# New places in the on-chip memory for the forms of x, the values and the heads' output of a hybrid decoder layer, and one form computed and split later

## The chip, the cores and the metric

The kernel runs on one core of a Trainium2 chip. Its time is the device time in microseconds of one execution. TensorE (PE) multiplies matrices; its loads of the stationary operand have a row of their own in the profile (PEld). VectorE (DVE), ScalarE (ACT) and GpSimd (POOL) do the elementwise work, and SyncE (SP) and GpSimd start transfers. Operands of a matmul lie in the on-chip memory (SBUF), in 128 partitions; a tile's place is a byte address that is the same in every partition. This text counts such addresses in units of 64 bytes, which are 16 floats.

## The reference

One decoder layer on 512 tokens with 16 learned tokens ahead, model width 1024. All weights of the first projection are one matrix `w_in`.

```python
u = rms_norm(h, norm_gain)
proj = u @ w_in
(rq, rk, rv, rg, gq, gk, gv, gg, glr, m_ret, m_gla) = jnp.split(proj, points, axis=-1)
rq, rk = rope(rq), rope(rk) * 256 ** -0.5               # 4 heads of 256
o_ret = head_group_norm(retention_chunked(rq, rk, rv)) * silu(rg)     # 4 heads of 512
log_a = log_sigmoid(glr @ w_gate_up + b_gate) / 16
o_gla = head_rms_norm(gla_chunked(gq, gk, gv, log_a)) * silu(gg)      # 4 heads: keys 128, values 256
merged = sigmoid(m_ret) * (o_ret @ w_branch_ret) + sigmoid(m_gla) * (o_gla @ w_branch_gla)
return rms_norm(h + merged @ w_out, final_norm_gain)[:, N_META:]
```

(Reshapes are left out, and the gains of the norms.) The result is 512 x 1024 in float32.

## The kernel before

**Products in three matmuls.** A float32 operand is split into a high part, which ScalarE makes by a cast (`split`, L154), and a low part, which VectorE makes by subtracting the high part from the value. A product of two operands is the sum of high by high, high by low and low by high: three matmuls with the same result tile (`mm3`, L189 to L193, and the inner loop of `quad`, L318).

**Seven products for eight.** `quad` computes a product of a 2x2 block matrix of x (two halves of tokens `th` by two halves of the width `kh`) with a 2x2 block of weights by seven block products. They are issued in the order 1, 2, 6, 7, 5, 4, 3 and use the forms A11, A12, S2, S3, S1, A22, S4 of x: three are blocks of x itself, and S1 to S4 are sums and differences of blocks. Each product is 24 matmuls: two halves of 128 columns, four blocks of depth, three matmuls each. With `rows=True` a form of x is the stationary operand and 256 columns of a weight are the moving one; this holds for `gv1`, `gg0`, `gg1`, `rg0` to `rg3`, `rv0` to `rv3` (gates and values of the heads) and `wo1` (a part of the output projection). With `rows=False` the weight is stationary and the form moves, 256 or, where the learned tokens go along, 264 columns; this holds for `rqk0` to `rqk3` and `gqk1` (queries and keys), `mr0`, `mr1`, `mg0`, `mg1` (merging gates) and `bg0`, `bg1` (the GLA branch, whose forms come from the GLA heads and not from x). The projections `gq0`, `gk0` and `gv0` are done with all eight products, and so are two other parts of the output projection, `wo0` and `wo2`, with the merged heads as stationary operand.

**Where the operands lie.** `xh` and `xl` hold the high and low parts of x, one tile per `kh`, shaped [128, 4, 2, 272]: four blocks of depth, two halves of tokens, 264 columns used of 272. A row (one block of depth) is 34 units of 64 bytes, and the second half starts 17 units behind the first. S1 to S4 lie in tiles `fh3` to `fh6` and `fl3` to `fl6` of [128, 4, 272], with rows of 17 units. A split weight is [128, 4, 256], rows of 16 units, in one of three buffers each for high and low (`whi`, `wlo`); raw weights come by transfers into six buffers. Values of a retention head are `vh` and `vl`, its gates `sg`, the scores `sh` and `sl`, its normed and gated output, transposed, `oh` and `ol`; the branch projection (`br`, 512 wide) has weights stationary and `oh`, `ol` moving. The merged heads `mh`, `ml` take over tiles that are free by then, and their forms those of `fh3` to `fl6`.

**Order.** A scheduler places each instruction on its engine, and the code fixes the order where it matters: `pin` ties each product on TensorE to the last one before it; `act` and `vec` do the same on ScalarE and VectorE; `after` names one predecessor. Stages are generators that `weave` interleaves, a step of the dense one (a product) with a step of another chain. `low` holds the last cast and subtraction of a weight. In `gla_g(0)` (the quad `gg0`) the GLA heads' chain of small matmuls runs between the products. The forms of x are made once, at the start: in `forget_gates` (from L754) S2 and S4 are cast, then all four low parts are subtracted.

Of the kernel before, what the change touches and what calls it, by code (L numbers as in the profile page):

```python
# [28 lines left out]
P = 128  # L29
D = 1024  # L30
T = 512
# [16 lines left out]
E_U, E_D, E_A, E_B, E_END, E_ND = range(6)  # L48
A11, A12, A22, S1, S2, S3, S4 = range(7)


# [57 lines left out]
def hybrid_kernel(ctx: ExitStack, tc: tile.TileContext, I, out: bass.AP):  # L109
# [18 lines left out]

    xh = [cp.tile([P, 4, 2, HW], F32R, tag=f"xh{i}", name=f"xh{i}") for i in range(2)]
    xl = [cp.tile([P, 4, 2, HW], F32R, tag=f"xl{i}", name=f"xl{i}") for i in range(2)]  # L130
    ah = {(th, kh): xh[kh][:, :, th] for th in range(2) for kh in range(2)}
    al = {(th, kh): xl[kh][:, :, th] for th in range(2) for kh in range(2)}
    fh = [ah[0, 0], ah[0, 1], ah[1, 1]]
    fl = [al[0, 0], al[0, 1], al[1, 1]]
    fh += [cp.tile([P, 4, HW], F32R, tag=f"fh{i}", name=f"fh{i}") for i in range(3, 7)]
    fl += [cp.tile([P, 4, HW], F32R, tag=f"fl{i}", name=f"fl{i}") for i in range(3, 7)]

# [27 lines left out]
    def act(ins):  # L165
        return queue("act", ins)

    def vec(ins):
        return queue("vec", ins)
# [493 lines left out]
    for n in range(NTB):  # L663
        act(nc.scalar.activation(xr[n], xr[n], AF.Square, accum_out=ss[:, n:n + 1]))
        if n == 2:
            for s in range(2):
# [14 lines left out]
                             rt.unsqueeze(2).to_broadcast([P, NTB + 1, P])))  # L681
    vec(nc.vector.scalar_tensor_tensor(u01, u00, -1.0, u01, op0=ALU.mult, op1=ALU.subtract))

    def form(i, x):
        act(nc.scalar.copy(fh[i][:, :, :HT], x))

        def rest():
            vec(nc.vector.tensor_sub(fl[i][:, :, :HT], x, fh[i][:, :, :HT].bitcast(F32)))

        return rest  # L690
# [40 lines left out]
    def forget_gates():  # L731
# [24 lines left out]
        next_weights(0)  # L756
        forms.append(form(S4, u01))
        for i in (2, 0, 1, 3):
            forms[i]()
        yield  # L760
        def values(p):
# [84 lines left out]
    def gla_g(p):  # L846
        sg = g1.tile([P, NTB, 512], F32, tag="gsg", name=f"gsg{p}")
        G["sg", p] = sg

        def evac(n, th, x, y):  # L850
            total(sg[:, 2 * th:2 * th + 2, n * 256:(n + 1) * 256], x, y)

        yield from quad((C_GG + p * 512, C_GG + p * 512 + 256), True, f"gg{p}", evac,
                        sooner=p == 0)

# [408 lines left out]
    def ret_g(h):  # L1264
        sg = rp.tile([P, NTB, 512], F32, tag="sg", name=f"sg{h}")
        R["sg", h] = sg
# [3 lines left out]
    def ret_v(h):  # L1270
        vh = rp.tile([P, NTB, 512], F32R, tag="vh", name=f"vh{h}")
        vl = rp.tile([P, NTB, 512], F32R, tag="vl", name=f"vl{h}")
        R["v", h] = vh, vl
# [23 lines left out]
    def ret_scores(h):  # L1297
        qh, ql, kh, kl = R["qk", h]
        dec = rp.tile([P, 2, T], F32, tag="dec", name=f"dec{h}")
        nc.sync.dma_start(dec, I["decay"][h])  # L1300
        sh = rp.tile([P, 1280], F32R, tag="sh", name=f"sh{h}")
        sl = rp.tile([P, 1280], F32R, tag="sl", name=f"sl{h}")
# [26 lines left out]
    def ret_attention(h):  # L1329
# [4 lines left out]
        if h == 0:  # L1334
            nc.gpsimd.memset(rp.tile([P, 16], F32, name="gap"), 0.0)
        oh, ol = [(rp if h < 3 else cp).tile([P, 4, T], F32R, tag=f"o{n}" if h < 3 else f"x{n}0", name=f"o{n}{h}")
                  for n in "hl"]
        R["o", h] = oh, ol
# [109 lines left out]
    for h in range(4):  # L1448
# [10 lines left out]
        else:  # L1459
            weave(run(ret_g(h), ret_v(h)), run(every(ret_rope(h), 3, 2, at if h else None), ret_scores(h)))  # L1460
    weave(gates_ret(), ret_attention(3))

    mh, ml = [[cp.tile([P, 4, T], F32R, tag=f"x{n}1", name=f"m{n}0"),
               rp.tile([P, 4, T], F32R, tag=("sg", "vl")[n == "l"], name=f"m{n}1")] for n in "hl"]
    sums = [[cp.tile([P, 4, 256], F32R, tag=f"f{n}{i}", name=f"ms{n}{i}") for i in range(3, 7)] for n in "hl"]
    mforms = [[m[0][:, :, :256], m[1][:, :, :256], m[1][:, :, 256:], *x] for m, x in zip((mh, ml), sums)]

# [37 lines left out]

    weave(ret_branches(), residual(), skip=14)


# [105 lines left out]
```

## Time and profile before

| | |
|---|---|
| median of 3 runs | 757.08 us (756.8 to 758.7) |
| profiled execution, its own time | 759.11 us |
| span of the profiled execution | 757.3 us |
| granted TensorE clock in it | 0.998 |
| TensorE busy | 748.2 us, 99%, 5595 matmuls |
| VectorE busy | 609.2 us, 80% |
| ScalarE busy | 450.4 us, 59% |
| GpSimd busy | 138.8 us, 18% |
| read from and written to device memory | 104.44 and 11.53 MB |

Engines work side by side, so the shares don't add up. A busy time of TensorE counts a matmul from its issue to its modelled end, and matmuls overlap: the mean duration of a 128x256 matmul is given as 281 ns while 24 of them pass in 2.75 to 2.85 us. How fast matmuls follow each other is therefore read from the chain of waits, whose rows give start, length and number (`x24`) of a run of instructions with one name. That chain goes back from the last instruction, at each step to what released it. The columns of a window are its bounds and length, then the busy time and number of instructions of PE, PEld, DVE, ACT and POOL, the granted clock, the DMA engines' share and GB/s.

### The profile page before, as it was taken

To read this page: it belongs to the slowest core of one execution; us is meant where nothing else is said; L and a number is where in the kernel's file an instruction comes from. 1 tells how busy PE (TensorE), PEld (TensorE's weight loads), DVE (VectorE), ACT (ScalarE), POOL (GpSimd) and SP (SyncE) were. 2 spreads that over 40 slices of the span, in tenths; PEclk is the share of its full clock that TensorE was granted. 3 is DMA by queue.
4 is the path that set the end of the run, shared out by engine and by line. 5 is a ranking of instruction groups with operands and counts; after the bars stand their busy time and mean duration, and the time that the engine had idled before them with its cause. 6 is when DMAs were issued, how large, how long until landed. Compare 5 with 4: busy or idle time off the path is not lost.

```text
span 757.3 us, 14065 instructions
## 1 busy us (share of the span) xinstructions
PE 748.2 (99%) x5595; PEld 701.3 (93%) x5595; DVE 609.2 (80%) x873; ACT 450.4 (59%) x764; POOL 138.8 (18%) x173
## 2 busy tenths in 40 slices
PE   9999999999999999999999999999999999999996
PEld 6799899999999999999989999989999999988996
DVE  6699877679897789789957688966787989775994
ACT  7897584666974466556546555646464756532562
POOL 2211110101221122110530100440011210111142
PEclk9999999999999999999999999999999999999999
DMA  9863421821589972733783562795476356687503
GB/s 301 286 141 78 118 63 50 195 85 57 130 182 272 305 165 88 168 112 133 199 249 117 120 159 86 204 223 136 130 166 145 107 144 189 227 194 210 128 29 112
DMA packets 100138, 117.42 MB, mean 155 GB/s; under 512 B 5732, under 2 KB 90852, under 8 KB 99816
## 3 DMA queue, kind: packets, MB, share of 16 engines
q1 hardware_dynamic: 79896, 88.19, 36.7%
q0 software_dynamic: 19888, 27.79, 20.3%
q8 instruction: 44, 0.72, 0.4%
q10 hardware_dynamic: 288, 0.53, 0.2%
q14 instruction: 22, 0.18, 0.1%
HBM read 104.44 MB, written 11.53 MB: 153 GB/s over the span
## 4 chain that ended last, share of the span: by engine, by line
PE 86%; DVE 6%; ACT 2%; DMA 2%; issue 2%; POOL 1%; POOLq 0%; DVEq 0%; ACTq 0%
PE rqk_b L318 6%; PE rv_b L318 6%; PE rg_b L318 6%; PE rqk_c L318 5%; PE br_p L193 3%; PE br_p L189 3%; PE br_p L192 3%; PE gg_b L318 3%; PE gv_p L643 3%; PE mg_b L318 3%; PE rv_c L318 3%; PE rg_c L318 3%; PE mr_b L318 2%; PE bg_b L318 2%; PE gg_c L318 2%
## 5 line engine op out<-in xcount | busy, mean ns | idle before, releaser
L189 PE MATMUL br_p<-oh,br_h 128*128 128x512 f32 x128 | 50.0, 390 | 0.0
L193 PE MATMUL br_p<-oh,br_l 128*128 128x512 f32 x128 | 50.0, 390 | 0.0
L192 PE MATMUL br_p<-ol,br_h 128*128 128x512 f32 x128 | 49.8, 389 | 0.0
L154 ACT CAST rv_h<-rv_w 128x1024 fp32r<-128x1024 f32 x24 | 25.3, 1052 | 27.2 <-DVE rv_w L372 9.6
L154 DVE TENSOR_TENSOR rv_l<-rv_w,rv_h 128x1024 fp32r<-128x1024 f32 x24 | 29.3, 1221 | 9.2 <-ACT rv_h L154 9.2
L154 DVE TENSOR_TENSOR rg_l<-rg_w,rg_h 128x1024 fp32r<-128x1024 f32 x20 | 24.4, 1220 | 8.3 <-ACT rg_h L154 8.3
L154 ACT CAST rg_h<-rg_w 128x1024 fp32r<-128x1024 f32 x20 | 21.0, 1052 | 15.6 <-PE br_p L192 6.0
L282 POOL DMA_DIRECT2D rqk_x<-in_w_in_dram x8 | 10.4, 1302 | 105.4 <-DVE rv_l L154 80.6
L193 PEld LDWEIGHTS br_p<-oh,br_l 128*128 128x128 f32 x128 | 24.0, 188 | 5.2
L192 PEld LDWEIGHTS br_p<-ol,br_h 128*128 128x128 f32 x128 | 24.0, 188 | 4.7
L189 PEld LDWEIGHTS br_p<-oh,br_h 128*128 128x128 f32 x128 | 24.1, 188 | 4.5
L154 ACT CAST rqk_h<-rqk_w 128x1024 fp32r<-128x1024 f32 x20 | 21.1, 1053 | 11.5 <-PE rqk_c L318 2.9
L154 ACT CAST br_h<-br_w 128x1024 fp32r<-128x1024 f32 x16 | 16.8, 1050 | 18.7 <-PE br_p L192 9.5
L154 DVE TENSOR_TENSOR rqk_l<-rqk_w,rqk_h 128x1024 fp32r<-128x1024 f32 x20 | 24.4, 1221 | 3.9 <-ACT rqk_h L154 3.8
L1354 ACT ACTIVATE on<-av,nm,g_r 128x512 f32<-128x512 f32 x16 | 12.5, 779 | 25.3 <-DVE nm L1352 25.3
L318 PE MATMUL rv_b<-rv_l,fh 128*128 128x256 f32 x96 | 27.1, 282 | 0.2 <-DVE rv_l L154 0.2
L318 PE MATMUL rqk_b<-fh,rqk_h 128*128 128x256 f32 (+1 forms) x96 | 27.2, 283 | 0.0
L318 PE MATMUL rqk_b<-fh,rqk_l 128*128 128x256 f32 (+1 forms) x96 | 27.1, 282 | 0.0
L318 PE MATMUL rqk_b<-fl,rqk_h 128*128 128x256 f32 (+1 forms) x96 | 27.1, 282 | 0.0
L318 PE MATMUL rg_b<-rg_h,fl 128*128 128x256 f32 x96 | 27.0, 281 | 0.0
L318 PE MATMUL rv_b<-rv_h,fl 128*128 128x256 f32 x96 | 27.0, 281 | 0.0
L318 PE MATMUL rg_b<-rg_l,fh 128*128 128x256 f32 x96 | 26.9, 280 | 0.0
(721 smaller groups left out, 3260.8 us busy)
## 6 DMA issues: line engine op xcount, KB each, us to landing
rv_w<-in_w_in_dram SPq DMA_DIRECT2D x16, 512.0 KB, 4.2
br_w<-in_w_branch_ret_dram SPq DMA_DIRECT2D x16, 512.0 KB, 3.4
rqk_w<-in_w_in_dram SPq DMA_DIRECT2D x12, 512.0 KB, 4.8
rg_w<-in_w_in_dram SPq DMA_DIRECT2D x12, 512.0 KB, 4.5
rqk_x<-in_w_in_dram SPq DMA_DIRECT2D x8, 512.0 KB, 4.0
rqk_x<-in_w_in_dram POOLq DMA_DIRECT2D x8, 512.0 KB, 8.0
rg_x<-in_w_in_dram SPq DMA_DIRECT2D x8, 512.0 KB, 3.7
rg_x<-in_w_in_dram POOLq DMA_DIRECT2D x8, 512.0 KB, 7.8
```

What stands on the lines that cost most here:

```text
L154: return nc.scalar.copy(hi, src), nc.vector.tensor_sub(lo, src, hi.bitcast(F32))
L189: m = nc.tensor.matmul(o, lh, rh, start=first, stop=False)
L192: nc.tensor.matmul(o, lh, rl, start=False, stop=False)
L193: m = nc.tensor.matmul(o, ll, rh, start=False, stop=last)
L282: x = nc.gpsimd.dma_start(t, block(0, 1), accum_op=ALU.add)
L318: m = nc.tensor.matmul(ps[t][:, :n] if wide else ps[t], l, r, start=first and j == 0, stop=kk == 3 and j == 2, skip_group_check=not fresh ...
L643: m = nc.tensor.matmul(pss[t], (al if j == 1 else ah)[t // 2, kh][:, k, c], (lo if j == 2 else hi)[:, kk, :], start=q == kk == j == 0, sto ...
L1354: nc.scalar.activation(on, ps, AF.Identity, scale=r, bias=nm)
```

## The change

The forms of x move into three pairs of tiles. `x0` (rows of 544 floats, 34 units) holds the first half of the width, both halves of tokens 272 floats apart, and form S4 in columns 288 to 543: it lies on the second half of tokens of that block of x, which is not read any more when S4 is made. `x1` (rows of 864 floats, 54 units) holds the second half of the width, halves 288 floats apart, and S1 behind them. `x2` (rows of 608 floats, 38 units) holds S2 and S3, each 288 wide. Two tiles that hold nothing (`gap0`, 16 floats, `gap1`, 112 floats) shift what follows. In the built program the parts and forms that the quads read start at even units and split weights still start at odd ones. S1 and S4 are now 256 wide, where they were 264.

`sg` and `vl` become 2304 and 2176 floats instead of 2048, `sh` is read from 64 floats (256 bytes) on, the memset of a 16-float gap goes and the tile stays without it, and the last head's `oh`, `ol` go into the tiles of `x2`, 112 floats in. The merged heads and their forms get the same rows as x.

Form S4 is not made in `forget_gates` any more. There only its float32 value is computed, after the other forms were split; its cast and its subtraction come in `gla_g(0)`, behind the fifth product of `gg0`, tied to the cast and the subtraction of the weights last split. TensorE's and SyncE's instructions and their order stay as they were.

```diff
--- before.py
+++ after.py
@@ -47,6 +47,7 @@
 SOFF = (0, 512, 896, 1152)
 E_U, E_D, E_A, E_B, E_END, E_ND = range(6)
 A11, A12, A22, S1, S2, S3, S4 = range(7)
+OH3 = 112
 
 
 def constants():
@@ -126,14 +127,22 @@
     nc.gpsimd.memset(one, 1.0)
 
 
-    xh = [cp.tile([P, 4, 2, HW], F32R, tag=f"xh{i}", name=f"xh{i}") for i in range(2)]
-    xl = [cp.tile([P, 4, 2, HW], F32R, tag=f"xl{i}", name=f"xl{i}") for i in range(2)]
+    def gap(pool, n, name):
+        pool.tile([P, n], F32, name=name)
+
+    gap(cp, 16, "gap0")
+    x0, x1, x2 = [[cp.tile([P, 4, w], F32R, tag=f"x{n}{i}", name=f"x{n}{i}") for n in "hl"]
+                  for i, w in enumerate((544, 864, 608))]
+    gap(cp, 112, "gap1")
+
+    def halves(t, w):
+        return t[:, :, :2 * w].rearrange("p k (t c) -> p k t c", t=2)
+
+    xh, xl = [[halves(a, HW), halves(b, 288)] for a, b in zip(x0, x1)]
     ah = {(th, kh): xh[kh][:, :, th] for th in range(2) for kh in range(2)}
     al = {(th, kh): xl[kh][:, :, th] for th in range(2) for kh in range(2)}
-    fh = [ah[0, 0], ah[0, 1], ah[1, 1]]
-    fl = [al[0, 0], al[0, 1], al[1, 1]]
-    fh += [cp.tile([P, 4, HW], F32R, tag=f"fh{i}", name=f"fh{i}") for i in range(3, 7)]
-    fl += [cp.tile([P, 4, HW], F32R, tag=f"fl{i}", name=f"fl{i}") for i in range(3, 7)]
+    fh, fl = [[a[0, 0], a[0, 1], a[1, 1], b[:, :, 576:832], c[:, :, :288], c[:, :, 288:576], z[:, :, 288:]]
+              for a, z, b, c in zip((ah, al), x0, x1, x2)]
 
     rt = cp.tile([P, NTB + 1], F32, name="rt")
     rneg = cp.tile([P, NTB + 1], F32, name="rneg")
@@ -679,13 +688,22 @@
 
     vec(nc.vector.tensor_mul(dg, ident.unsqueeze(1).to_broadcast([P, NTB + 1, P]),
                              rt.unsqueeze(2).to_broadcast([P, NTB + 1, P])))
-    vec(nc.vector.scalar_tensor_tensor(u01, u00, -1.0, u01, op0=ALU.mult, op1=ALU.subtract))
-
-    def form(i, x):
-        act(nc.scalar.copy(fh[i][:, :, :HT], x))
+
+    def form(i, x, prev=None):
+        w = 256 if i in (S1, S4) else HT
+        h, l, x = fh[i][:, :, :w], fl[i][:, :, :w], x[:, :, :w]
+        y = nc.scalar.copy(h, x)
+        if prev:
+            after(y, prev[0])
+        else:
+            act(y)
 
         def rest():
-            vec(nc.vector.tensor_sub(fl[i][:, :, :HT], x, fh[i][:, :, :HT].bitcast(F32)))
+            y = nc.vector.tensor_sub(l, x, h.bitcast(F32))
+            if prev:
+                after(y, prev[1])
+            else:
+                vec(y)
 
         return rest
 
@@ -754,9 +772,9 @@
         parts["gk0", 0] = wsplit([P, 4, 256], "gk0_0")
         forms.append(form(S2, u00))
         next_weights(0)
-        forms.append(form(S4, u01))
-        for i in (2, 0, 1, 3):
+        for i in (2, 0, 1):
             forms[i]()
+        vec(nc.vector.scalar_tensor_tensor(u10, u00, -1.0, u01, op0=ALU.mult, op1=ALU.subtract))
         yield
         def values(p):
             for t in (2 * p, 2 * p + 1):
@@ -850,8 +868,13 @@
         def evac(n, th, x, y):
             total(sg[:, 2 * th:2 * th + 2, n * 256:(n + 1) * 256], x, y)
 
-        yield from quad((C_GG + p * 512, C_GG + p * 512 + 256), True, f"gg{p}", evac,
-                        sooner=p == 0)
+        products = quad((C_GG + p * 512, C_GG + p * 512 + 256), True, f"gg{p}", evac, sooner=p == 0)
+        if p == 0:
+            yield from islice(products, 4)
+            next(products)
+            form(S4, u10, low)()
+            yield
+        yield from products
 
     def gla_qk(p):
         q = gp.tile([P, 2, T], F32, tag="gq", name=f"gq{p}")
@@ -1262,14 +1285,14 @@
         yield
 
     def ret_g(h):
-        sg = rp.tile([P, NTB, 512], F32, tag="sg", name=f"sg{h}")
+        sg = rp.tile([P, 2304], F32, tag="sg", name=f"sg{h}")[:, :2048].rearrange("p (b c) -> p b c", b=NTB)
         R["sg", h] = sg
         yield from quad((C_RG + h * 512, C_RG + h * 512 + 256), True, f"rg{h}", rows_into(sg, AF.Silu),
                         ahead=h % 3 == 0, behind=R.get(("pow", h - 1)))
 
     def ret_v(h):
         vh = rp.tile([P, NTB, 512], F32R, tag="vh", name=f"vh{h}")
-        vl = rp.tile([P, NTB, 512], F32R, tag="vl", name=f"vl{h}")
+        vl = rp.tile([P, 2176], F32R, tag="vl", name=f"vl{h}")[:, :2048].rearrange("p (b c) -> p b c", b=NTB)
         R["v", h] = vh, vl
 
         def meta(psm):
@@ -1298,7 +1321,7 @@
         qh, ql, kh, kl = R["qk", h]
         dec = rp.tile([P, 2, T], F32, tag="dec", name=f"dec{h}")
         nc.sync.dma_start(dec, I["decay"][h])
-        sh = rp.tile([P, 1280], F32R, tag="sh", name=f"sh{h}")
+        sh = rp.tile([P, 1344], F32R, tag="sh", name=f"sh{h}")[:, 64:]
         sl = rp.tile([P, 1280], F32R, tag="sl", name=f"sl{h}")
         sm = rp.tile([P, T], F32R, tag="sm", name=f"sm{h}")
         R["s", h] = sh, sl, sm
@@ -1332,9 +1355,12 @@
         vm, sg = R["vm", h], R["sg", h]
 
         if h == 0:
-            nc.gpsimd.memset(rp.tile([P, 16], F32, name="gap"), 0.0)
-        oh, ol = [(rp if h < 3 else cp).tile([P, 4, T], F32R, tag=f"o{n}" if h < 3 else f"x{n}0", name=f"o{n}{h}")
-                  for n in "hl"]
+            gap(rp, 16, "gap7")
+        if h < 3:
+            oh, ol = [rp.tile([P, 4, T], F32R, tag=f"o{n}", name=f"o{n}{h}") for n in "hl"]
+        else:
+            oh, ol = [cp.tile([P, 2432], F32R, tag=f"x{n}2", name=f"o{n}{h}")[:, OH3:OH3 + 4 * T]
+                      .rearrange("p (k c) -> p k c", k=4) for n in "hl"]
         R["o", h] = oh, ol
 
         def values(ib):
@@ -1460,10 +1486,12 @@
             weave(run(ret_g(h), ret_v(h)), run(every(ret_rope(h), 3, 2, at if h else None), ret_scores(h)))
     weave(gates_ret(), ret_attention(3))
 
-    mh, ml = [[cp.tile([P, 4, T], F32R, tag=f"x{n}1", name=f"m{n}0"),
-               rp.tile([P, 4, T], F32R, tag=("sg", "vl")[n == "l"], name=f"m{n}1")] for n in "hl"]
-    sums = [[cp.tile([P, 4, 256], F32R, tag=f"f{n}{i}", name=f"ms{n}{i}") for i in range(3, 7)] for n in "hl"]
-    mforms = [[m[0][:, :, :256], m[1][:, :, :256], m[1][:, :, 256:], *x] for m, x in zip((mh, ml), sums)]
+    def rows4(t, o, w, c):
+        return t[:, o:o + 4 * w].rearrange("p (k c) -> p k c", k=4)[:, :, :c]
+
+    m0 = [cp.tile([P, 3456], F32R, tag=f"x{n}1", name=f"m{n}0") for n in "hl"]
+    mh, ml = [[rows4(t, 0, 544, T), rows4(rp.tile([P, w], F32R, tag=g, name=f"m{n}1"), o, 544, T)]
+              for n, t, g, w, o in zip("hl", m0, ("sg", "vl"), (2304, 2176), (16, 0))]
 
     def merged(k, t):
         return [m[k // 4][:, k % 4, t * P:(t + 1) * P] for m in (mh, ml)]
@@ -1504,6 +1532,13 @@
         nc.sync.dma_start(hs[1], I["x"][:, 512:].rearrange("(t p) d -> p t d", p=P))
 
     weave(ret_branches(), residual(), skip=14)
+
+    mforms = []
+    for n, m, t in zip("hl", (mh, ml), m0):
+        s23 = cp.tile([P, 2176], F32R, tag=f"x{n}0", name=f"ms{n}0")
+        s4 = cp.tile([P, 2432], F32R, tag=f"x{n}2", name=f"ms{n}2")
+        mforms.append([m[0][:, :, :256], m[1][:, :, :256], m[1][:, :, 256:], rows4(t, 2176, 288, 256),
+                       rows4(s23, 0, 256, 256), rows4(s23, 1024, 256, 256), rows4(s4, 0, 288, 256)])
 
 
 ```

On ScalarE, in `forget_gates` near the start, before (`fh_85` is S2's high part, `fh_87` S4's, `gk_0_h` a weight, `fg_e` the forget gates):

```order
L743 CAST fg_wz<-la 128x512
L744 ACTIVATE gvm_110<-gvm_s,rt 16x512
L685 CAST fh_85<-u_130 128x4x264
L154 CAST gk_0_h<-gk_w_468 128x1024
L685 CAST fh_87<-u_131 128x4x264
L785 ACTIVATE fg_e_510<-z_508 128x512
```

And now, first there, and then in `gg0`, where S4 (`xh_81`) went (`gg_5_h` and `gg_4_h` are the weights of its fifth and sixth product, `lah` the log gates, `gkm` and `gkt` masks and keys of the GLA heads):

```order
L761 CAST fg_wz<-la 128x512
L762 ACTIVATE gvm_106<-gvm_s,rt 16x512
L695 CAST xh_85<-u_126 128x4x264
L163 CAST gk_0_h<-gk_w_463 128x1024
L803 ACTIVATE fg_e_504<-z_502 128x512
```

```order
L163 CAST gg_5_h<-gg_x_729 128x1024
L695 CAST xh_81<-u_126 128x4x256
L343 COPY gg_x_862<-gg_b 128x512
L979 ACTIVATE gkm_872<-gm_869 128x16
L979 ACTIVATE gkm_878<-gm_875 128x16
L163 CAST lah_970<-la 128x256
L163 CAST gg_4_h<-gg_w_727 128x1024
L969 COPY gkt_919<-gc_911 128x128
```

S4's cast left the place between `gk_0_h` and the forget gates and stands between `gg_5_h` and a copy out of PSUM; `gg_4_h`, which stood right behind that copy, stands three rows later.

On VectorE, at the same place in `gg0`, before and now (`stb` are score blocks under their mask, `xl_82` is S4's low part, `gsg` the gates that `gg0` adds up):

```order
L154 TENSOR_TENSOR gg_5_l<-gg_x_735,gg_5_h 128x1024
L942 COPY_PREDICATED stb_725<-gmask,gc_927 128x128
L154 TENSOR_TENSOR lal_975<-la,lah_974 128x256
L154 TENSOR_TENSOR gg_4_l<-gg_w_733,gg_4_h 128x1024
L154 TENSOR_TENSOR gg_3_l<-gg_w_736,gg_3_h 128x1024
```

```order
L163 TENSOR_TENSOR gg_5_l<-gg_x_729,gg_5_h 128x1024
L702 TENSOR_TENSOR xl_82<-u_126,xh_81 128x4x256
L163 TENSOR_TENSOR lal_971<-la,lah_970 128x256
L163 TENSOR_TENSOR gg_4_l<-gg_w_727,gg_4_h 128x1024
L163 TENSOR_TENSOR gg_3_l<-gg_w_730,gg_3_h 128x1024
```

S4's subtraction now stands between `gg_5_l` and `lal`. In `forget_gates` (L688 before) VectorE has one subtraction less in its row of four.

## The prediction

> **What bounds the kernel now.** I read the busy times first, then the waits of TensorE, the chain of waits, and the windows in which that chain leaves TensorE. From the page:
>
> ```profile
> span 757.3 us, 14065 instructions
> PE 748.2 (99%) x5595; PEld 701.3 (93%) x5595; DVE 609.2 (80%) x873; ACT 450.4 (59%) x764; POOL 138.8 (18%) x173
> PE 86%; DVE 6%; ACT 2%; DMA 2%; issue 2%; POOL 1%; POOLq 0%; DVEq 0%; ACTq 0%
> ```
>
> TensorE is busy for all but 9 us at an undiminished clock (1.00 in the windows further down), and 86% of the chain is matmuls. Its waits past the warm-up are small; from the list of waits (us in all, times, longest), the largest, and the one by the last value projection:
>
> ```profile
> PE bg_b L318 <- DVE gs L1129: 0.9, 1, 0.9
> ...
> PE rv_b L318 <- DVE rv_l L154: 0.2, 1, 0.2
> ```
>
> So the kernel gets shorter only by fewer matmuls or by matmuls that follow each other faster. The change leaves TensorE's instructions and their order alone; it moves the addresses of their operands. The question is whether an address shows in the trace. It does, in the chain (start us, us, what; x24 is one of the seven products of a `quad`, in the order 1, 2, 6, 7, 5, 4, 3):
>
> ```profile
> 253.67 2.93 PE rqk_b L318 x24
> ...
> 268.18 2.90 PE rqk_c L318 x24
> 271.08 2.84 PE rqk_b L318 x24
> 273.92 2.85 PE rg_b L318 x24
> ...
> 285.30 2.84 PE rg_b L318 x24
> 288.14 2.75 PE rg_c L318 x24
> ```
>
> The sixth product of `rg` takes 2.75 us and the others 2.84 or 2.85, for the same 24 matmuls of 128x128 by 128x256. Nothing else differs between them but where their operands lie. The gap recurs in another quad of that kind, and in the output's stage there is a third figure:
>
> ```profile
> 138.97 2.84 PE gv_b L318 x24
> 142.26 2.75 PE gv_c L318 x24
> ...
> 734.30 2.80 PE wo_c L318 x24
> 737.10 2.88 PE wo_b L318 x24
> ```
>
> The sixth product is the one with A22, the second half of tokens. In before's layout `xh` and `xl` have rows of 34 units of 64 bytes and the halves 272 floats, 17 units, apart; in the built program the first half starts at an odd unit, the second at an even one, the forms `fh3`–`fh6` have rows of 17 units and so change between odd and even from row to row, and every split weight (rows of 16 units) is odd. A22 is the only form that is even throughout. My reading: **where the moving operand of a matmul and the stationary operand loaded beside it lie at opposite parities of 64 bytes, the next matmul starts sooner.** By the starts that is (2.84 − 2.75)/24 = 3.8 ns a matmul.
>
> Which operand moves matters. With weights moving (`rows=True`, above) the moving side has one parity. In the gates `mr` and `mg` x moves, and in the GLA branch (`bg`) another form does:
>
> ```profile
> 245.40 2.72 PE bg_b L318 x24
> 248.12 2.83 PE bg_c L318 x24
> ...
> 370.21 2.84 PE mg_b L318 x24
> 375.82 2.83 PE mg_c L318 x24
> ```
>
> Here A22's product at 375.82 gains 0.01 us only. Its x rows are 34 units apart, so even, but a multiple of four only every second time. The `bg` product at 2.72, also with x moving, has forms at one constant even place, opposite to the weights; the one at 2.83, A22 there, reads a piece laid out otherwise. So x that moves seems to need a constant place.
>
> **The change, part by part.** (a) All forms of x become even. The quads with weights moving are `gg0`, `gv1`, `gg1`, `rg0`–`rg3`, `rv0`–`rv3`: 11 quads with 6 products each that are not A22's, 66 products. From 2.845 to 2.74 (between `bg`'s 2.72 and A22's 2.75, which holds a few matmuls before the faster beat sets in): 66 × 0.105 = **6.9 us**. Bounds: 0, and 66 × 0.125 = 8.3.
>
> (b) The output stage `wo` has 15 blocks of 24 matmuls with the merged forms, stationary too (4, 7 and 4), now all even. They take 2.80 to 2.88, by the starts 2.85 in the mean: 15 × 0.11 = **1.7 us**. Bounds 0 and 2.2.
>
> (c) Where x moves, the new rows of 34, 54 and 38 units alternate as A22's do now, so I give every product what A22's has: `mr`/`mg` 24 × 0.012 = 0.3; in `rqk` and `gqk1` (5 quads) the four 264 wide go from 2.90–2.93 to A22's 2.90, 20 × 0.015 = 0.3, and the two others from 2.845 to 2.83, 10 × 0.015 = 0.15. Together **0.75 us**. Below: 0. Above: 59 products × 0.11 = 6.5, if they fell to `bg`'s 2.72.
>
> (d) The 512-wide branch matmuls, of which `vl`, `sg`, the scores and the last head's `o` are shifted by 256 bytes:
>
> ```profile
> 356.28 0.23 PE br_p L189
> 356.96 0.23 PE br_p L189
> 361.85 0.23 PE br_p L189
> 362.54 0.23 PE br_p L189
> ```
>
> Three matmuls take 0.68 in one block and 0.69 in another. By the starts, 9 of the 32 blocks of 12 matmuls are in the slower beat, 4 ns a matmul more: 9 × 12 × 4 ns = **0.4 us** if all go to the faster one; 0 if none.
>
> (e) Form S4, in ScalarE's cast and VectorE's subtraction, moves from the forget gates into `gg0`. Durations and the gaps at its new place:
>
> ```profile
> 39.94 1.07 ACT L685 CAST fh<-u 128x1056 fp32r<-128x1056 f32 x1
> 41.21 4.76 DVE L688 TENSOR_TENSOR fl<-u,fh 128x1056 fp32r<-128x1056 f32 x4
> 68.69 0.59 ACT L334 COPY gg_x<-gg_b 128x512 f32<-128x512 f32 x1 [0.64 <-PE gg_b L318]
> 77.87 0.82 PE gg_c L318 x7
> 82.93 0.35 PE gg_b L318 x3
> ```
>
> The cast (1.07) lands on ScalarE behind `gg_5_h`, the subtraction (4.76/4 = 1.19) on VectorE behind `gg_5_l`, near 68 to 71 us. ScalarE is idle for 0.64 us there. The last product, which alone reads S4, starts at 82.93, over 10 us later. Queued behind on VectorE are `lal` and `gg_4_l`, the latter for the product that starts near 77.9. I count it **0**; without cover it costs 1.19 + 1.07 − 0.64 = 1.6. The early place loses the same work: gain 0 to 1. The memset taken from GpSimd is nothing (GpSimd is 18% busy).
>
> Gross: 6.9 + 1.7 + 0.75 + 0.4 = 9.75 us.
>
> **What is lost again.** A faster TensorE gains nothing where it then waits. The chain and the windows (us; busy time of PE, PEld, DVE, ACT, POOL; clock; DMA):
>
> ```profile
> 601.67 0.28 DVE ol L495
> 615.62 2.98 PE rv_b L318 x23
> 706.94 0.60 DVE sigr L1444
> 730.96 3.34 PE wo_b L318 x24
> 219.78 8.92 DMA og<-og1gq
> 586.00:609.00 23.00, 23.00 (x211) 22.26 (x213) 23.00 (x32) 15.95 (x27) 4.93 (x5) 1.00 0.37 115
> 707.00:742.00 35.00, 34.81 (x288) 34.31 (x287) 32.79 (x42) 21.89 (x46) 13.98 (x20) 1.00 0.12 37
> ```
>
> From 586 to 609 VectorE has no gap at all and carries the chain to 615.62, where TensorE already waits 0.2: `rg3`'s gain (6 × 0.105) is lost, **0.6**. From 706.94 to 730.4 VectorE carries it again: what `wo`'s first 8 blocks gain falls away, 8 × 0.11 = **0.9**. In the GLA stage the chain runs through ScalarE, VectorE and a transfer of 8.92 us; its three quads earn 18 × 0.105 = 1.9, of which I take under half as lost, **0.8** (0 to 1.9). Sum 2.3, against 14% of 9.75 = 1.4 if the chain's foreign share were spread evenly.
>
> Net 9.75 − 2.3 = 7.45. The profiled execution took 759.11, 1.8 above its span of 757.3; the median 757.08 lies 0.2 below that span. So the span should be 749.9 and the median **749.6 us**.
>
> One rule speaks against all this. The Trainium skill, "SBUF — State Buffer", section "🔬 SBUF: two separate sides", knows contention between engines only on the port that VectorE and GpSimd share; TensorE waits on nobody. By it the address of an operand has no part in the pace, and the time stays near 757. The rows of 2.75 beside 2.84 speak against its being the whole truth, since the instructions are alike; no run yet moves an address alone.
>
> **Rivals.** *Starved* (0.17): TensorE speeds up by the 9.75, but VectorE, ScalarE and transfers pace more of it. The window 586–609 speaks for it; against it, leads elsewhere, as the waits quoted come to 1.1 us. With double the loss, 4.6 to 6: 752 to 753.5.
>
> *x moving is fast too* (0.10): constant evenness is enough and (c) pays its 6.5. For: `bg` at 2.72. Against: A22's 2.83 in `mg`, whose rows are already even. Net 749.6 − 5.7 less some loss: about 744.
>
> *Addresses do nothing* (0.07): product six is faster because of its accumulation or its place in the order, and the change doesn't do what it says. Against: in `mg` the sixth is not faster, and in `bg` it is the slowest. Time 757, or 758 with (e).
>
> *A fixed pairing is slower* (0.05): the beat depends on the exact distance of the two operands, and the new places are like those of `wo_b` at 2.88, its first operands also in one fixed relation. Place: all 66 products on TensorE; price 66 × (2.88 − 2.845) = 2.3 us, and 15 × 0.03 more; with (e)'s 1.6 about 761. It decides from the point where the new products exceed 2.845 on average. Against: A22's product has just the new relation, x even with rows 34 apart, weights odd, and has 2.75.
>
> **How the numbers follow.** The forecast has 0.61. Its terms reach from 66 × 0.09 = 5.9 with 3.5 lost of 8.5 (5 net, 752) to 8.3 + 2.2 + 0.75 + 0.4 less 1.5 (10.1 net, 747). To leave out no more than 2 in 10, the range takes in *starved* and most of *x moving*: 744.5 to 754.5. A measurement of this kernel can tell no less than 0.3%, 2.3 us, from no change: 754.8 and below is faster. Forecast, *x moving* and nearly all of *starved* are faster: 0.87; *addresses do nothing* and the tail of *starved* same: 0.09; the last rival slower: 0.04.
>
> **What would show it.** Right: all seven products of `rg1` or `rv1` at 2.72 to 2.76 in the chain; `wo` at 2.72 to 2.76; `mg` at 2.83 throughout; `br` 0.68 for three; more waits of TensorE on VectorE near 590 to 610 and 715 to 730; the share of the chain on TensorE down by a few points. Wrong: `rg` still at 2.84 (parity is not the cause), or at 2.74 with TensorE's busy time 10 us shorter and the span hardly so (starved), or `mg` and `rqk` at 2.73; or `gg_4_l` released late near 78 us, which would give (e) a price.

## The result and the profile after

The change takes 750.24 us in the median of 6 runs (749.79 to 752.13) against 757.86 of the kernel before (6 runs, 756.8 to 758.97): a ratio of 0.9905 with a 95% interval of 0.9889 to 0.9921, 7.6 us less. The forecast was 749.6. The profiled execution took 750.33 us, its span is 748.6.

The page of the changed kernel, its first rows and the chain's shares:

```profile
span 748.6 us, 14064 instructions
PE 738.6 (99%) x5595; PEld 691.7 (92%) x5595; DVE 607.7 (81%) x873; ACT 450.3 (60%) x764; POOL 137.5 (18%) x172
PE 89%; DVE 7%; issue 2%; ACT 1%; POOL 0%; POOLq 0%; DVEq 0%; ACTq 0%
```

The same 5595 matmuls keep TensorE busy for 738.6 us where it was 748.2; VectorE and ScalarE do what they did. Where the 9.6 us went shows in the chain of waits (start us, us, what), at the quad `rg0` and the product ahead of it, then in `mg0` and in the output stage:

```profile
264.81 2.91 PE rqk_c L327 x24
267.72 2.80 PE rqk_b L327 x24
270.52 2.73 PE rg_b L327 x24
273.25 2.72 PE rg_a L327 x24
...
281.41 2.72 PE rg_b L327 x24
284.13 2.72 PE rg_c L327 x24
...
345.77 2.83 PE mg_b L327 x24
365.27 2.83 PE mg_b L327 x24
...
726.22 2.72 PE wo_c L327 x24
728.94 2.72 PE wo_b L327 x24
```

All products of `rg0` now take 2.72 or 2.73, a little under the 2.75 that A22's alone took before, and the output's 2.80 and 2.88 became 2.72. Where x moves, `mg` is at 2.83 and `rqk` 264 wide at 2.91. The list of waits has three rows of TensorE on VectorE, at the places where the forecast had gains lost. Two are new; the one of `rv_b` had 0.2 before:

```profile
PE rg_c L327 <- DVE rg_l L163: 0.6, 1, 0.6
PE wo_c L327 <- DVE wo_l L163: 0.5, 1, 0.5
PE rv_b L327 <- DVE rv_l L163: 0.5, 1, 0.5
```

The row `PE bg_b <- DVE gs` with 0.9 us is gone, and that is not the change's doing: it is gone too in the run below that has every address of before, and in three variants of the changed kernel, which leave the GLA branch alone, it is there with 0.9, 0.5 and 0.7. So of the 8.7 us between the two profiled spans about 0.9 is chance. Another 0.6 arises in the first matmuls, at 6 to 7 us, behind the first loads; there the run with before's addresses also starts 0.3 earlier. What is left, 7.2, is near the 7.6 of the medians.

### The profile page after: what moved, and what is told of

Same layout as the page of the kernel before. It is cut to its first block, busy times and chain, and to the rows that moved or that the text cites. A ratio compares the mean times of both kernels' runs of the same rounds, so it can differ in the third digit from the quotient of the medians.

```text
span 748.6 us, 14064 instructions
## 1 busy us (share of the span) xinstructions
PE 738.6 (99%) x5595; PEld 691.7 (92%) x5595; DVE 607.7 (81%) x873; ACT 450.3 (60%) x764; POOL 137.5 (18%) x172
## 4 chain that ended last, share of the span: by engine, by line
PE 89%; DVE 7%; issue 2%; ACT 1%; POOL 0%; POOLq 0%; DVEq 0%; ACTq 0%
PE rqk_b L327 6%; PE rv_b L327 6%; PE rg_b L327 5%; PE rqk_c L327 5%; PE br_p L201 4%; PE br_p L202 4%; PE br_p L198 4%; PE gg_b L327 3%; PE mg_b L327 3%; PE mr_b L327 3%; PE gv_p L652 3%; PE rv_c L327 3%; PE bg_b L327 2%; PE rg_c L327 2%; PE gk_p L437 2%
## 5 line engine op out<-in xcount | busy, mean ns | idle before, releaser
L163 ACT CAST rv_h<-rv_w 128x1024 fp32r<-128x1024 f32 x24 | 25.3, 1053 | 25.3 <-DVE rv_w L381 10.4
L327 PE MATMUL rqk_b<-xh,rqk_h 128*128 128x264 f32 (+1 forms) x128 | 36.2, 283 | 0.0
L327 PE MATMUL rqk_b<-xh,rqk_l 128*128 128x264 f32 (+1 forms) x128 | 36.1, 282 | 0.0
L327 PE MATMUL rqk_b<-xl,rqk_h 128*128 128x264 f32 (+1 forms) x128 | 36.0, 281 | 0.0
L327 PE MATMUL rv_b<-rv_l,xh 128*128 128x256 f32 x128 | 35.5, 277 | 0.5 <-DVE rv_l L163 0.5
L163 DVE TENSOR_TENSOR rv_l<-rv_w,rv_h 128x1024 fp32r<-128x1024 f32 x24 | 29.3, 1221 | 8.1 <-ACT rv_h L163 8.1
L327 PE MATMUL rv_b<-rv_h,xh 128*128 128x256 f32 x128 | 35.8, 280 | 0.0
L327 PE MATMUL rv_b<-rv_h,xl 128*128 128x256 f32 x128 | 35.4, 277 | 0.0
L327 PE MATMUL rg_b<-rg_h,xh 128*128 128x256 f32 x128 | 35.4, 277 | 0.0
L327 PE MATMUL rg_b<-rg_h,xl 128*128 128x256 f32 x128 | 35.4, 276 | 0.0
L327 PE MATMUL rg_b<-rg_l,xh 128*128 128x256 f32 x128 | 35.4, 276 | 0.0
L163 DVE TENSOR_TENSOR rg_l<-rg_w,rg_h 128x1024 fp32r<-128x1024 f32 x20 | 24.4, 1220 | 8.1 <-ACT rg_h L163 8.1
L163 ACT CAST rg_h<-rg_w 128x1024 fp32r<-128x1024 f32 x20 | 21.0, 1052 | 15.6 <-PE br_p L201 5.9
L163 ACT CAST rqk_h<-rqk_w 128x1024 fp32r<-128x1024 f32 x20 | 21.0, 1052 | 11.8 <-PE rqk_c L327 2.9
```

What stands on the lines that cost most here:

```text
L163: return nc.scalar.copy(hi, src), nc.vector.tensor_sub(lo, src, hi.bitcast(F32))
L327: m = nc.tensor.matmul(ps[t][:, :n] if wide else ps[t], l, r, start=first and j == 0, stop=kk == 3 and j == 2, skip_group_check=not fresh ...
```

## The experiments

**Pairs of places.** A kernel without the layer, that only issues matmuls at chosen places.

```diff
-  (the whole layer)
+    k3 = (0, 16, 32)
+    for m in range(8):
+        for s in range(8):
+            series(f"c{L[m]}x{L[s]}", lambda i: m + k3[i % 3], lambda i: s + k3[i // 2 % 3], 256, 24)
...
```

(The first line stands for all that goes. `series` issues 24 matmuls, here with the moving operand at `m` and the stationary one at `s`, in units of 64 bytes; `k3` adds multiples of 16 units. Further series have 264 and 512 columns, or rows that alternate.)

> This kernel leaves out the whole layer: it only issues series of 24 matmuls of 128x128 by 128x256 (12 of 512 columns, 48 with alternating rows), each with the moving operand at one place m and the stationary one at one place s, counted in units of 64 bytes (letters a = 0, b = 1, ...; in a result's name cbxd stands m = 1 and s = 3). Parity theory: all 32 pairs of opposite parity follow each other at about 113.3 ns (24 in 2.72 us), all 32 of equal parity at 117 to 120 ns (2.81 to 2.88 us). Rival, the distance m - s modulo four decides: only 16 of the 64 pairs are fast, as the GLA branch has 2.72 us at distance 3 modulo four and 2.83 us at distance 1. Rival, addresses do nothing: all 64 series take the same time within 0.02 us.

The mean distance from one matmul's start to the next in a series, from the ninth on, in ns; places from 4 on repeat the table to 0.1, so 16 of its 64 entries are shown:

```
moving \ stationary    0      1      2      3
0                    120.0  117.7  118.7  117.8
1                    117.7  120.0  113.3  118.7
2                    118.7  117.7  120.0  117.7
3                    117.8  118.7  117.7  120.0
```

In the chain, four of these series, then series of 48 in which one operand is at one place and the other goes to and fro by one row. In their names h means that the stationary operand does so, g that the moving one does; the second letter is the row, e for 34 units and g for 36, which keeps the place modulo four:

```profile
37.67 2.88 PE cbxb L44 x24
40.55 2.73 PE cbxc L44 x24
43.28 2.84 PE cbxd L44 x24
...
60.24 2.82 PE ccxb L44 x24
...
301.31 5.66 PE geaxd L44 x48
306.97 5.47 PE heaxd L44 x48
312.44 5.61 PE gecxd L44 x48
318.05 5.46 PE hecxd L44 x48
...
340.55 5.45 PE hgaxd L44 x48
```

So addresses do count, with a period of four units, 256 bytes. Equal places cost 120.0, places two apart 118.7: no series of the table with equal parity is faster than that. At odd distances it is 117.7 or 113.3. But only one of the eight odd pairs of the table, moving 1 and stationary 2, was at 113.3, and by distance alone it should have had company (0 and 1, 2 and 3 have the same one and are at 117.7). Both simple theories were wrong in part: in the table opposite parity is needed for 113.3 and does not ensure it. Nor does the pair of places alone decide: moving 3 against stationary 0 passes at 117.8 in the table, and at 113.3 in the last row of the chain (5.45 for 48). The series with rows tell more: the same two operands at moving 3, stationary 0 and 2 in turn reach 113.3 after some eight matmuls (5.47 and 5.46 for 48), while with a moving operand that alternates they don't (5.66, 5.61). The split fits the layer: there x as stationary operand alternates and gained, and x as moving operand alternates and did not.

**Weights moved by 64 bytes.** The change, with x where it is and weights at even places too.

```diff
-    gap(cp, 112, "gap1")
+    gap(cp, 96, "gap1")
```

> The changed kernel with the empty tile gap1 96 floats instead of 112: all split weights and what lies behind them move by 64 bytes, x and its forms stay where the change put them, so x and weights now have equal parity everywhere. Parity theory: the products of the quads with weights moving go from 2.72 back to 2.84 to 2.88 us each, 77 products x 0.12 = 9 us, some of it in stretches that VectorE sets anyway: 756 to 760 us, slower than the change by 1 % or more. Rival, x only has to lie at even units whatever the weights do: 2.72 us stays and the time is 750 us. The blocks of the output projection that read the second half of the merged heads, which move along with the weights, should stay fast in both theories.

Measured: 759.73 us, 1.0023 of before (1.0014 to 1.0032): all of the gain is gone, and a little more. The chain at `rg0` and in `mg0`:

```profile
278.37 2.85 PE rg_b L327 x24
281.22 2.85 PE rg_c L327 x24
284.07 2.86 PE rg_b L327 x24
286.93 2.85 PE rg_c L327 x24
...
358.25 2.85 PE mg_b L327 x24
```

2.85 throughout, A22's product too, which had 2.75 before. The blocks of the output that read the second half of the merged heads, which moved along, stayed at 113.3 to 115.3 ns in the same execution, while the others went to 118.3 to 119.1. What sets the pace is the parity of one operand against the other, not x at an even place by itself.

**Form S4 late, alone.** Before, with only the part of the diff in `forget_gates`, `form` and `gla_g`; every address as before.

```diff
-        forms.append(form(S4, u01))
-        for i in (2, 0, 1, 3):
+        for i in (2, 0, 1):
             forms[i]()
+        vec(nc.vector.scalar_tensor_tensor(u10, u00, -1.0, u01, op0=ALU.mult, op1=ALU.subtract))
...
+            form(S4, u10, low)()
```

> The kernel before, every operand at its old address, with only form S4 cast and subtracted later, behind the fifth product of gg0. My theory: no measurable change, 757 us within 1 us; TensorE's last product of gg0 doesn't wait. Rival, the late split delays the GLA heads' chain: 758 to 759 us, with TensorE waiting on gg_4_l near 78 us. Rival, a part of the gain of 7.6 us came from this move and not from addresses: 754 to 756 us.

Measured: 757.9 us, 0.9999 of before (0.999 to 1.0008). The move costs and brings nothing; no row for `gg` is among TensorE's waits. In the changed kernel the cast fell on ScalarE without an idle gap ahead, as its timeline shows, and the product that waits for the next weights started on time:

```profile
66.34 1.05 ACT L163 CAST gg_h<-gg_x 128x1024 fp32r<-128x1024 f32 x1
67.29 1.04 ACT L695 CAST xh<-u 128x1024 fp32r<-128x1024 f32 x1
68.24 0.57 ACT L343 COPY gg_x<-gg_b 128x512 f32<-128x512 f32 x1
```

**Rows by four units.** The change, with a form at one place modulo four in all four blocks of depth.

```diff
-                  for i, w in enumerate((544, 864, 608))]
+                  for i, w in enumerate((576, 832, 576))]
```

(and the three tiles that share their places, cut to 3328 and 2304 floats)

> The changed kernel with rows of 36, 52 and 36 units in the three pairs of x tiles instead of 34, 54 and 38, so that a form lies at one place modulo four units in all four blocks of depth: A11, A12, S1 and S2 at 0, A22, S3 and S4 at 2, weights still at 3. If moving x only needs a constant even place, the 63 products with x moving gain up to 0.11 us each (2.83 to 2.72; 264 wide 2.90 to 2.80): about 744 us. If it needs distance 3 modulo four, as in the GLA branch, only the three forms at 2 gain, 27 x 0.11 = 3 us: 747 us. If the same distance rule holds for stationary x, the products with the four forms at 0 stay at 2.72 and those with the three at 2 go to 2.84, a loss of 33 x 0.12 = 4 us: 750 to 751 us. If rows do nothing: 750 us.

Measured: 752.66 us, 0.9929 of before (0.9916 to 0.9941), 2.4 us slower than the change. The chain at `rg0` and, 130 us later, at `rv1`:

```profile
271.04 2.83 PE rg_b L327 x24
273.87 2.83 PE rg_a L327 x24
...
282.35 2.72 PE rg_b L327 x24
285.07 2.72 PE rg_c L327 x24
287.79 2.72 PE rg_b L327 x24
...
418.07 2.72 PE rv_a L327 x24
420.79 2.72 PE rv_b L327 x24
...
429.42 2.83 PE rv_c L327 x24
```

Nothing in the expectation fits: the same form is at 2.83 in one quad and at 2.72 in another. With both operands at one place the pace has two values, 113.3 and 117.8, and mostly keeps the one it has: `rv_c` at 429.42 follows two matmuls of another kind and is slow, the product ahead of them was fast. Where x moves, `mg` stayed at 117.7 to 117.9 ns a matmul, but four of the 14 products of `mr` passed at 113.3 to 113.8, and the last product of `rqk` and `gqk1`, 256 wide, at 113.5 to 114.5 in four of five quads. So the constant place that I thought moving x lacked does help, now and then; it ensures nothing. In the change, where moving x alternates, no product was under 116.5. And the rows that alternate, which this run took away, are what I now think carries the stationary x of the change to 113.3 each time; the next run tests it.

**Layouts.** Again without the layer: products in the layer's order, with 16 layouts and three things ahead of each.

```diff
-  (the whole layer)
+    cfgs = [(xw, dx, ww, dw) for xw in (34, 36) for dx in (0, 2) for ww in (16, 18) for dw in (0, 2)]
+    for c, (xw, dx, ww, dw) in enumerate(cfgs + cfgs[:1]):
+        for b, (xb, wb) in enumerate(((0, 3), (2, 3))):
+            for e in "xyz":
+                product(f"r{L[c]}{L[b]}{e}", True, xw, dx, ww, dw, xb, wb, 256, e)
...
```

(The first line stands for all that goes. `xw` is the length of x's rows and `dx` the offset of its low part against the high one, `ww` and `dw` the same of the weights, in units of 64 bytes. The lines left out do the same with x moving.)

> This kernel leaves out the whole layer: it issues products of 24 matmuls in the order of the layer's own (two halves, four blocks of depth, high by high, high by low, low by high), with the first letter r where x is stationary and m or n where it moves (n: 264 columns), the second letter a layout, the third a place of x (a: x at 0, b: x at 2 modulo four units; weights at 3), the last what comes ahead (nothing, one matmul of 512 columns, two of 128). Layouts: rows of x of 34 or 36 units, low part of x 0 or 2 units off the high one, rows of weights of 16 or 18, low weight 0 or 2 off; a to h have 34, i to p 36, q repeats a. Theory from the pairs and from the kernel with rows of 36: opposite parity allows the beat of 113.3 ns and a stationary operand that alternates between 0 and 2 modulo four brings TensorE into it, whatever comes ahead; so r with rows of 34 (2.72 us after the first), and m where the weights alternate by rows of 18 or by their low part, with x at one place; m with x alternating and the weights fixed stays at 2.80 to 2.83 us. Rival: the beat is a matter of what comes ahead, and the three entries of one layout differ by 0.1 us as often as two layouts do.

Means in ns from the seventh matmul on; six values are two places of x by three things ahead:

```
layout (rows of x, low x off, rows of weights, low weight off)    r: x stationary                       m: x moving                          n: 264 moving
a  34, 0, 16, 0 (the change)   113.3 113.3 113.4 113.3 114.0 114.0   117.7 117.2 117.2 116.6 116.6 117.2   121.1 121.0
e  34, 2, 16, 0                113.3 114.8 113.4 113.8 113.8 113.4   117.9 117.8 116.7 117.7 117.8 117.8   116.6 116.6
i  36, 0, 16, 0                113.4 113.3 113.4 117.8 117.8 117.8   113.4 117.8 117.8 117.8 117.8 113.3   119.8 120.6
k  36, 0, 18, 0                117.6 117.8 117.8 116.8 117.8 117.7   113.3 113.4 113.4 113.4 113.4 113.4   120.4 120.6
q  (a again, at the end)       115.1 116.6 115.1 114.0 114.0 114.0   117.1 116.8 117.8 116.6 116.6 117.2   121.2 121.0
```

Two rows of the chain, of layout k with x stationary and moving:

```profile
426.15 2.82 PE rkax L59 x24
...
435.09 2.73 PE mkax L59 x24
```

Layout k turns the roles round: weights that alternate and are stationary, x that moves at one place; now m is fast in all six and r is not. With i, where nothing alternates, both have both values. So the theory holds in this form: **opposite parity allows 113.3 ns; a stationary operand that alternates between 0 and 2 modulo four (or 1 and 3), against a moving one at one place, brings TensorE to it; and without that it depends on what came before.** Not fully: q is layout a with the first place at 115 to 117, because the beat is found late there, after 9 to 18 matmuls; all six of its series then keep 113.3. The first entries of a are no like test, since the first matmuls of these products were issued ahead of the rest of them. And the theory's other way to alternate, by a low part two units off at rows that don't alternate, works only in part: with weights so off (36, 0, 16, 2) m ends at 113.3 in four of six series, with x so off (36, 2, 16, 0) r does in four of six, and the others stay near 119. Where the moving operand alternates, no mean of 256 columns was under 115.4. And one thing that was not looked for: in layout e the 264-wide product falls from 121 to 116.6. Of the eight 264-wide series with rows of 34 and x's low part two off six do; with rows of 36 none does.

**Scores and heads' output back.** The change, with the 256 bytes between scores and values, and between output and weights, undone.

```diff
-        sh = rp.tile([P, 1344], F32R, tag="sh", name=f"sh{h}")[:, 64:]
+        sh = rp.tile([P, 1344], F32R, tag="sh", name=f"sh{h}")[:, :1280]
...
-            gap(rp, 16, "gap7")
+            gap(rp, 80, "gap7")
```

> The changed kernel with the scores' high parts back by 256 bytes and the heads' output forward by 256, so that both have their distances of before (0 or 8 modulo 16 units) to what they meet. Theory: the branch matmuls fall back by 0.2 to 0.4 us of 87, the rest stays: span 748.6 to 749.1. Rival, the shift of values and output carries a larger part of the gain: span 750 or more.

One run: 751.92 us, span 750.2. All but 0.3 us of the 1.6 us more arises at one place, the first matmuls of the last product of `bg0`, behind a transfer; 0.9 of it stands in this kernel's list of waits:

```profile
PE bg_b L327 <- DVE gs L1152: 0.9, 1, 0.9
```

The branch matmuls took 227.2 ns in the mean, as in the change; before it was 227.7. So neither expectation: the 0.2 us that `br` gained is not from this offset, and the offset shows nothing at all. The pairs could have told it: their 512-wide series have 228.8, 233.2, 233.4 and 226.6 ns with the moving operand at 0 to 3 against stationary 3, and repeat to 0.2 when the moving operand goes on by four units, so that 256 bytes are a full period. (The last head's place, which this run leaves, had 226.6 ns before as well.) What made the difference from before I did not settle; the slower beat appears in some blocks of 12 in each kernel.

**Weights moved by 128 bytes.** Parities opposite as in the change, distances modulo four changed.

```diff
-    gap(cp, 112, "gap1")
+    gap(cp, 80, "gap1")
```

> The changed kernel with gap1 at 80 floats, so the split weights and what lies behind move by two units of 64 bytes against x: parities stay opposite, the distances modulo four change places. Parity theory: no change against the change itself, 749.5 to 751 us, the rg products at 2.72 to 2.75. Rival, the exact distance decides: some of the forms fall to 2.83, 752 to 757 us.

Measured: 751.49 us (4 runs), 0.9912 of before (0.9895 to 0.9928), not to be told from the change. The matmuls of the eleven quads average 114.0 ns, in the change 114.2, before 117.8. This doesn't part the two distances: the rows of x alternate by two units, so each form is one and three units from the weights in turn, in either kernel, and the move only swaps the turns. That swap costs the quads nothing. The branch matmuls of the last head, whose weights moved against its output, went from 226.6 to 233.5 ns, 0.7 us.

**Low parts off.** What layout e suggests, in the changed kernel.

```diff
...
+        for n in "hl":
+            x.append(cp.tile([P, 4, w], F32R, tag=f"x{n}{i}", name=f"x{n}{i}"))
+            if n == "h":
+                gap(cp, 32, f"gaph{i}")
...
-    gap(cp, 112, "gap1")
+    gap(cp, 144, "gap1")
```

> The changed kernel with the low parts of x and of its forms two units of 64 bytes off the high ones modulo four (32 empty floats between the two tiles of each pair, and so many behind them that the weights keep their place); nothing else moves against its neighbours but the last head's low output. From the layouts: with rows of 34 and the low part two off, 264 columns of moving x take 116.6 ns in place of 121, stationary x stays at 113.3 to 114.8, 256 columns of moving x stay at 117.7. So the 592 matmuls of 264 columns in rqk and gqk1 save 592 x 4.4 ns = 2.6 us, their products going from 2.90 to 2.80; some of it is lost in the stretches that VectorE sets: 748 us, about 2 us below the change. Rival, what the layouts showed for 264 columns depended on what came ahead: rqk stays at 2.90 and the time at 750 to 751 us. Rival, stationary x loses the fast beat in part, 1 ns on 1850 matmuls: 752 us.

Measured: 749.34 us (5 runs), 0.9891 of before (0.9872 to 0.9909): 0.9 us below the change, which the intervals don't separate. In the products themselves the gain is there. The chain at `rqk1`, where these products were 2.90 in the change:

```profile
320.75 2.84 PE rqk_c L331 x24
325.21 2.81 PE rqk_b L331 x24
330.31 2.82 PE rqk_c L331 x24
```

The 600 matmuls of 264 columns average 117.9 ns, after 121.1: 1.9 us earned. By the medians about half was not kept. Ahead of `rg0`, where TensorE now arrives earlier still, the chain of this kernel goes through a transfer and then VectorE, 26 us in all, and `rg0`'s own gain is mostly lost (0.15 us kept, where the change kept 0.77):

```profile
258.76 9.55 DMA rg_x<-in_w_in_dram
269.96 1.13 DVE rg_l L167
...
283.59 1.15 DVE rg_l L167
284.78 2.92 PE rg_c L331 x23
```

And `br` took 0.35 us more, two thirds of it at the last head, whose low output moved as well. By its median this is the fastest kernel seen here.

## Why the prediction was right, and where not

The place and the size held, and the mechanism in part: addresses set the pace, and equal parity is slow, but the reason given is half of what the runs show, and that the new layout had the other half was luck. By its terms, earned time being the difference of mean pitch times the number of matmuls:

```
term                                    forecast   measured
(a) eleven quads, weights moving          6.9      117.8 -> 114.2 ns x 1848 = 6.65
(b) output stage                          1.7      118.2 -> 113.5 x 192, 118.8 -> 113.8 x 168 = 1.75
(c) x moving                              0.75     0.39 (mr, mg) + 0.26 (264) + 0.30 (256 of rqk) = 0.95
(d) 512 wide                              0.4      227.7 -> 227.2 x 384 = 0.18
(e) S4 later                              0        0 (alone: ratio 0.9999)
gross                                     9.75     9.5
lost: rg3 and rv3                         0.6      1.1
lost: output stage                        0.9      0.9
lost: GLA stage                           0.8      0.35
net                                       7.45     7.1
```

The losses are read from how much earlier the same matmul starts in the trace of after. At the first matmul of `rg3` that is 7.93 us, at its largest within `rg3` 8.49, at the end of `rv3` 7.86, though the two quads earned 1.08 in pitch. In the output stage it goes from 7.95 to 8.78 where 1.75 were earned. The waits of 0.6, 0.5 and 0.5 above stand at these places and are the larger part of the losses. The forecast had `rg3`'s gain fall away and forgot `rv3`'s, which the same backlog of VectorE governs; and it took too much for the GLA stage. That the two misses nearly cancel is luck too. The bound above for (c) has a slip that changes nothing else: 63 products have x moving, not 59, which would make it 6.9 and not 6.5.

What was wrong is in the reasons. "x that moves seems to need a constant place" is no promise: with the rows by four `mg` is at a constant place and stays at 117.8, and only some products of `mr` and `rqk` get faster. What was read from `bg` at 2.72 was one of the two values that a pair of constant places can have. The forecast for (c) was right because it took A22's own rows and not that sentence. The bold sentence on parity is half the rule: the pairs show that opposite parity also goes with 117.7, and the rows by four and the layouts that the alternating rows of 34, 54 and 38 units, which the prediction knew only as a handicap where x moves, are what makes (a) and most of (b) reliable. Not all of (b): the merged forms S2 and S3 have rows of 256 floats, 16 units, and so lie at one place, not in rows like x's; they passed at 113.3 all the same, S3 after six slower steps. With constant rows of x, which it took for the better ones where x moves, the kernel was 2.4 us slower. Term (d) was mis-sized, 0.18 for 0.4, and its cause does not hold, since undoing the offset changed nothing.

Of the rivals, *addresses do nothing* fell with the weights moved by 64 bytes: the same instructions in the same order, 9.5 us apart. The Trainium skill, "TensorE: Matmul & The Clock Gate", section "Step-by-step: what each phase is for", gives TensorE a read port each for the moving operand and for the next stationary one, so that loading does not slow the running matmul; the pairs at 113.3 and 120.0 ns, alike but for 64 bytes, show a dependence of 6% on the two places that this leaves no room for, and the measurement decides; why it is so, no run shows. *A fixed pairing is slower* did not come, as the new products are at 2.72; 2.85 in all products is what equal parity gives. *x moving is fast too* would have needed other rows, those of layout k, which cost the stationary x its gain. *Starved* is true in part and was in the sum.

## What to carry to other kernels

When the same matmuls pass at two paces in one trace, compare where their operands lie before looking for a wait: here the start of the moving operand against that of the stationary one (no run tells whether it is the one in use or the one loaded for the next matmul), in units of 64 bytes, was worth 4 to 7 ns of 118 to 120 on each matmul of 256 columns in float32r. Put them at opposite parity, let the stationary one alternate between two places two units apart from row to row while the moving one keeps its place, and check the pace in the chain, since a pair of fixed places can settle at either value. Count a gain in matmul pace only up to the next engine that is full: 2.4 of 9.5 us earned fell away in three stretches that VectorE or a transfer sets.

## What the runs showed of the hardware that was not expected

The pace of back-to-back matmuls depends on both operands' places modulo 256 bytes: 120.0 ns at equal places, 118.7 at two units, 117.7 or 113.3 at one or three (256 columns). It has memory: with both operands fixed at opposite parity (layout i), the same 24 matmuls run at 113.3 or 117.8 ns depending on what preceded them. It is no chance of the execution: before and the run with S4 late alone, which share all addresses, keep the same distance of 1.30 to 1.36 us, matmul by matmul, from 254 us to the end. And 264 columns, 3% more than 256, can run at 116.6 ns, faster than many of 256, when high and low parts of the moving operand lie two units apart and its rows are 34 units long; why, these runs don't tell.
